# Up stage of a conv FFN: block products for the prompt alone, the sample tokens plainly

## The chip, the cores and the metric

The kernel runs on one core of a Trainium2 chip. The metric is the device time of one execution in microseconds. The kernel before took 1247.82 us (median of three executions, 1247.18 to 1248.13).

## The reference, cut to what matters

One layer of a streaming encoder: a mixer (gated MLP and latent attention), a layer norm, a gated feed-forward part with a causal convolution of width 3, a layer norm. There are 1024 prompt tokens and 8 x 16 = 128 sample tokens, all in float32. The change lies in the product with `w_up`, 1024 rows by 2 x 2816 columns, over all 1152 tokens:

```python
def conv_ffn(x, conv_past, w_up, w_conv, b_conv, w_down):
    up = jnp.einsum('bsd,df->bsf', x, w_up)          # D_MODEL 1024 -> 2 * D_FF = 5632
    padded = jnp.concatenate([conv_past, up], axis=1)
    conv = b_conv
    for k in range(CONV_W):
        conv = conv + w_conv[k] * padded[:, k:k + s_len]
    a, g = jnp.split(conv, 2, axis=-1)
    out = jnp.einsum('bsf,fd->bsd', jax.nn.silu(a) * g, w_down)
```

For the prompt `conv_past` is zero, for the samples it comes as an input. `x` here is the output of the first layer norm.

## The kernel before, in words

**Precision.** Every float32 operand of a large product is split into a high part (rounded by ScalarE, ACT, into the type float32r) and a low part (VectorE, DVE, subtracts: `split`, L59 to L61). A product is then three matmuls: high x high, high x low, low x high.

**Stages.** First the latent attention's projections and the attention (until about 260 us), then the gated MLP (until about 380), then the output projection with the first layer norm (`a4`, L819: nine tiles of 128 tokens, tile 8 holds the samples), then the up stage, then the down stage with the last layer norm.

**From the norm to the up stage.** `a4(t)` leaves the normalised tile t in `yt`; `c4(t)` (L841) transposes it on TensorE (eight transposes, L847) and ACT scales it into `hT` (L855), so that the hidden dimension lies on the partitions. In the loop over t (L940) `c4(t - 1)` stands behind `a4(t)`.

**The up stage.** It goes over 22 strips (L1078). Strip i makes 128 columns of the value half (Ua) and the 128 columns of the gate half that belong to them (Ug): a 2 x 2 block matrix of weights (rows of `w_up` in halves r; Ua or Ug) times a 2 x 2 block matrix of activations (`hblk(q, r, c)`: row half r, token half c of block q). Instead of eight block products it makes seven, in the manner of Strassen and Winograd, from sums and differences of blocks. The products have the numbers 1 to 7. `build_h` (L865) makes the activation operand of a product, once for the whole stage; the ones for 5, 6 and 4 go through one scratch block `Tc`, one after another. `build_w` (L896) makes the weight operand in each strip: a sum or difference on DVE (5, 6, 7, 3), then the split. `product_mm` (L922) runs a product's twelve matmuls: four slices of 128 of the hidden dimension, three matmuls each (L932 to L934). Three PSUM accumulators take the products: X (1, then 6, 7 and 4 on top), Y (2), Z (5, then 3). After each product the state of the accumulator is taken out into U: copied by ACT (1, 5, 6, 4; L1033) or added by DVE (2, 7, 3; L1031).

Before, all 1152 tokens go through the products in two blocks q of 576 tokens, each in two halves of NH = 288 columns: 7 x 2 x 12 matmuls of 288 columns a strip. The samples are the last 128 columns of block 1. The weights' operands have six buffers, so most of a strip's weights are built one strip ahead. In strip 0 the order of products is written out by hand (L1083): four products of block 0, then the two blocks in turn; three products of block 0 (`begun`, L951) are put behind `a4(8)`.

**After a strip.** The convolution of strip i (`conv`, L1035: one pass on ACT, two on DVE, for Ua and Ug), a Silu and the gate product run in pieces between the products of strip i + 1 (`pend`, L1093). The result goes to DRAM (`ad`) and comes back in the down stage. `load_down` (L1063) loads and splits a down operand into the buffers of activation operands that are done with (`ring`), the first four of them during the last strip.

**What sets the order.** The kernel's text gives each engine a stream; a planner with its own idea of durations orders the instructions of each engine, in program order among those it takes for ready, unless `keep_in_program_order` (`pin`) holds them. At run time an engine's queue is in fixed order. A buffer that is taken again waits for its last readers. `raw` tiles of weights have three buffers, U has three, PSUM has eight banks (A 3, B 2, C 1, D 2).

Of the kernel before, what the change touches and what calls it, by code (L numbers as in the profile page):

```python
# [42 lines left out]
def trunk(tc, a, o):  # L43
# [738 lines left out]
    for pl in reversed(g3):  # L782
# [58 lines left out]
    def c4(t):  # L841
        yt = yt_.pop(t)
        for g in range(2):
            tb = bank("B")
            for kk in range(4):
                k = 4 * g + kk
                pe.transpose(tb[:, kk * P:(kk + 1) * P], yt[:, k * P:(k + 1) * P], ident)  # L847
            for kk in range(4):
                k = 4 * g + kk
                lo = t * P  # L850
                while lo < (t + 1) * P:
                    q, at0 = divmod(lo, 2 * NH)
                    n = min((t + 1) * P - lo, 2 * NH - at0)
                    c0 = kk * P + lo - t * P
                    act.activation(hT[q][:, k, at0:at0 + n], tb[:, c0:c0 + n], AF.Identity,  # L855
                                   bias=ln1[:, 1, k:k + 1], scale=ln1[:, 0, k:k + 1])
                    lo += n

    STEPS = (1, 2, 5, 6, 7, 3, 4)
    bops = {}  # L860

    def hblk(q, r, c):
        return hT[q][:, 4 * r:4 * r + 4, c * NH:(c + 1) * NH]

    def build_h(pl, q, s):  # L865
        T = Tc[q]
        if s == 1:
            src = hblk(q, 0, 0)
        elif s == 2:
            src = hblk(q, 1, 0)  # L870
        elif s == 5:
            src = T
            dve.tensor_tensor(T, hblk(q, 0, 1), hblk(q, 0, 0), ALU.subtract)
        elif s == 6:
            src = T
            dve.tensor_tensor(T, hblk(q, 1, 1), T, ALU.subtract)
        elif s == 7:
            src = hblk(q, 0, 1)
            dve.tensor_tensor(src, hblk(q, 1, 1), src, ALU.subtract)
        elif s == 3:  # L880
            src = hblk(q, 1, 1)
        else:
            src = T
            dve.tensor_tensor(T, hblk(q, 1, 0), T, ALU.subtract)
        b = pl.tile([P, 2, 4, NH], F32R, tag=f"b{q}{s}", name=f"b{q}{s}")
        split(b[:, 0], b[:, 1], src)
        bops[q, s] = b
# [8 lines left out]
    def build_w(i, s):  # L896
        A = [[wraw[i][r][:, 512 * c:512 * (c + 1)] for c in range(2)] for r in range(2)]
        if s == 1:
            src = A[0][0]
        elif s == 2:  # L900
            src = A[0][1]
        elif s == 5:
# [19 lines left out]
    def product_mm(i, s, q, hold=lambda x: x):  # L922
        w, h = wops[i, s], bops[q, s]
        key = "Y" if s == 2 else "Z" if s in (5, 3) else "X"
        first = s in (1, 2, 5)
        if first:
            acc[i, q, key] = bank({"X": "A", "Y": "B", "Z": "D"}[key])
        b = acc[i, q, key]
        for k in range(4):
            lh, ll, rh, rl = w[:, 0, k], w[:, 1, k], h[:, 0, k], h[:, 1, k]  # L930
            o_ = b[:, :NH]
            hold(pe.matmul(o_, lh, rh, start=first and k == 0, stop=False, skip_group_check=not first))  # L932
            hold(pe.matmul(o_, lh, rl, start=False, stop=False, skip_group_check=not first))  # L933
            hold(pe.matmul(o_, ll, rh, start=False, stop=k == 3, skip_group_check=not first))  # L934
        return b

    wups = []
    bop0 = None
    begun = {}
    for t in range(TT + 1):  # L940
# [17 lines left out]
        if t == 6:  # L958
# [55 lines left out]
    def out_parts(U, q, c, b):  # L1014
        t0 = (2 * q + c) * NH
        n0 = min(NH, SEQ - t0)
        l = [(U[:, 2 + t0:2 + t0 + n0], b[:, :n0])]
        if n0 < NH:
            l.append((smp_cols(U)[:, :, 2:], b[:, n0:NH].rearrange("p (b s) -> p b s", b=NB)))
        return l  # L1020

    def product(i, s, q):
        b = begun.pop((i, s, q), None)
        if b is None:
            b = product_mm(i, s, q)
# [3 lines left out]
        for dst, src in out_parts(U, q, c, b):  # L1029
            if add:  # L1030
                dve.tensor_tensor(dst, dst, src, ALU.add)  # L1031
            else:
                act.activation(dst, src, AF.Copy)  # L1033
# [27 lines left out]
    ring = [bops[q, s] for s in STEPS for q in range(2)]  # L1061
# [273 lines left out]
```

## Time and profile before

| | us |
|---|---|
| median of three executions | 1247.82 |
| the profiled execution's own time | 1248.44 |
| its span, first to last instruction | 1246.7 |
| TensorE busy | 1227.5 (98%) |
| VectorE busy | 844.6 (68%) |
| ScalarE busy | 533.1 (43%) |
| GpSimd busy | 97.7 (8%) |
| first matmul of the up stage | 469.5 |
| last matmul of the up stage | 972.3 |

The span is 1.7 us shorter than the execution's own time. A matmul's duration in the profile is longer than the distance to the next one, since matmuls overlap in TensorE; a stretch in which TensorE is "busy" all the time may still run faster or slower. In the rows, PE is TensorE, PEld its weight loads, DVE VectorE, ACT ScalarE, POOL GpSimd, SP the engine that issues most DMAs. A group's row has line, engine, operation, output and inputs, shapes and count, then busy time, mean duration in ns, and idle time before it with what ended it.

### The profile page before, as it was taken

To read this page: it belongs to the slowest core of one execution; us is meant where nothing else is said; L and a number is where in the kernel's file an instruction comes from. 1 tells how busy PE (TensorE), PEld (TensorE's weight loads), DVE (VectorE), ACT (ScalarE), POOL (GpSimd) and SP (SyncE) were. 2 spreads that over 40 slices of the span, in tenths; PEclk is the share of its full clock that TensorE was granted. 3 is DMA by queue.
4 is the path that set the end of the run, shared out by engine and by line. 5 is a ranking of instruction groups with operands and counts; after the bars stand their busy time and mean duration, and the time that the engine had idled before them with its cause. 6 is when DMAs were issued, how large, how long until landed. Compare 5 with 4: busy or idle time off the path is not lost.

```text
span 1246.7 us, 19600 instructions
## 1 busy us (share of the span) xinstructions
PE 1227.5 (98%) x7737; PEld 1137.6 (91%) x7737; DVE 844.6 (68%) x1642; ACT 533.1 (43%) x1098; POOL 97.7 (8%) x229
## 2 busy tenths in 40 slices
PE   7999999999999999999999999999999999999997
PEld 7999999889988888999999999999999888888886
DVE  5767888665558568877777677786777794552445
ACT  5335656542134546645445454454545330220332
POOL 0110003200000001111000010000100000000021
PEclk9999999999999999999999999999999999999999
DMA  7201103541043330221222212121233762421012
GB/s 251 83 21 40 33 22 116 165 161 52 1 142 109 134 112 18 104 73 71 90 71 71 74 70 90 63 79 73 71 106 131 291 245 97 145 68 41 12 57 85
DMA packets 35853, 116.47 MB, mean 93 GB/s; under 512 B 5120, under 2 KB 6272, under 8 KB 35760
## 3 DMA queue, kind: packets, MB, share of 16 engines
q1 hardware_dynamic: 30176, 95.19, 22.1%
q0 software_dynamic: 5584, 20.02, 4.3%
q8 instruction: 61, 1.00, 0.3%
q14 instruction: 32, 0.26, 0.1%
HBM read 90.46 MB, written 24.74 MB: 92 GB/s over the span
## 4 chain that ended last, share of the span: by engine, by line
PE 97%; ACT 1%; DVE 1%; DMA 1%; issue 0%; SPq 0%; ACTq 0%; DVEq 0%
PE A L934 8%; PE A L933 7%; PE A L932 7%; PE A L72 7%; PE A L73 7%; PE A L74 7%; PE D L72 7%; PE D L73 7%; PE D L74 7%; PE D L934 4%; PE D L933 4%; PE D L932 4%; PE B L72 2%; PE B L73 2%; PE B L74 2%; PE B L934 2%
## 5 line engine op out<-in xcount | busy, mean ns | idle before, releaser
L932 PE MATMUL A<-b,wu 128*128 128x288 f32 x704 | 207.6, 296 | 0.5 <-DVE U L1031 0.4
L933 PE MATMUL A<-b,wu 128*128 128x288 f32 x704 | 207.9, 296 | 0.0
L934 PE MATMUL A<-b,wu 128*128 128x288 f32 x704 | 206.0, 298 | 0.0
L932 PEld LDWEIGHTS A<-b,wu 128*128 128x128 f32 x704 | 132.4, 188 | 1.0 <-DVE U L1031 0.6
L933 PEld LDWEIGHTS A<-b,wu 128*128 128x128 f32 x704 | 132.8, 189 | 0.0
L934 PEld LDWEIGHTS A<-b,wu 128*128 128x128 f32 x704 | 131.1, 188 | 0.0
L934 PE MATMUL D<-b,wu 128*128 128x288 f32 x352 | 104.8, 298 | 0.0
L932 PE MATMUL D<-b,wu 128*128 128x288 f32 x352 | 104.1, 296 | 0.0
L933 PE MATMUL D<-b,wu 128*128 128x288 f32 x352 | 104.0, 295 | 0.0
L60 ACT ACTIVATE wu<-sc 128x512 fp32r<-128x512 f32 x66 | 41.8, 633 | 138.2 <-PE A L934 105.0
L60 ACT ACTIVATE b<-cbox 128x1024 fp32r<-128x1024 f32 (+1 forms) x40 | 25.6, 676 | 142.7 <-PE B L73 42.2
L61 DVE TENSOR_TENSOR wu<-sc,wu 128x512 fp32r<-128x512 f32 x66 | 46.2, 701 | 46.5 <-ACT wu L60 45.0
L1039 DVE SCALAR_TENSOR_TENSOR cbox<-U,raw,cbox 128x1168 f32<-128x1168 f32 x44 | 63.0, 1431 | 9.4 <-ACT cbox L1038 9.3
L933 PEld LDWEIGHTS D<-b,wu 128*128 128x128 f32 x352 | 66.4, 189 | 0.1
L932 PEld LDWEIGHTS D<-b,wu 128*128 128x128 f32 x352 | 66.1, 188 | 0.3 <-ACT b L60 0.3
L934 PEld LDWEIGHTS D<-b,wu 128*128 128x128 f32 x352 | 66.1, 188 | 0.0
L1040 DVE SCALAR_TENSOR_TENSOR cbox<-U,raw,cbox 128x1168 f32<-128x1168 f32 x44 | 63.0, 1431 | 0.8
L1038 ACT ACTIVATE cbox<-U,raw 128x1168 f32<-128x1168 f32 x44 | 60.0, 1363 | 7.3 <-DVE U L1031 7.1
L60 ACT ACTIVATE wu<-raw 128x512 fp32r<-128x512 f32 x66 | 41.6, 631 | 47.5 <-PE D L934 23.6
L1033 ACT ACTIVATE U<-A 128x288 f32<-128x288 f32 (+2 forms) x154 | 53.0, 368 | 17.5 <-PE A L934 17.5
L61 DVE TENSOR_TENSOR wu<-raw,wu 128x512 fp32r<-128x512 f32 x66 | 45.0, 685 | 14.5 <-ACT wu L60 14.5
L932 PE MATMUL B<-b,wu 128*128 128x288 f32 x176 | 52.1, 296 | 1.7 <-ACT hbox L855 1.7
(449 smaller groups left out, 3419.9 us busy)
## 6 DMA issues: line engine op xcount, KB each, us to landing
raw<-in_w_up SPq DMA_DIRECT2D x44, 512.0 KB, 3.2
ad<-cbox POOLq DMA_DIRECT2D x22, 584.0 KB, 3.1
cbox<-ad SPq DMA_DIRECT2D x22, 584.0 KB, 6.1
raw<-in_w_down SPq DMA_DIRECT2D x22, 512.0 KB, 5.7
xr<-in_xT SPq DMA_DIRECT2D x14, 512.0 KB, 4.1
y<-in_x SPq DMA_DIRECT2D x9, 512.0 KB, 3.6
nd<-y SPq DMA_DIRECT2D x9, 512.0 KB, 2.6
raw<-in_w_uv_in SPq DMA_DIRECT2D x8, 512.0 KB, 4.0
```

The source lines that it names most:

```text
L60: act.activation(hi, src, AF.Copy)
L61: dve.tensor_tensor(lo, src, f(hi), ALU.subtract)
L72: pe.matmul(out, lh, rh, start=first, stop=False)
L73: pe.matmul(out, lh, rl, start=False, stop=False)
L74: pe.matmul(out, ll, rh, start=False, stop=last)
L932: hold(pe.matmul(o_, lh, rh, start=first and k == 0, stop=False, skip_group_check=not first))
L933: hold(pe.matmul(o_, lh, rl, start=False, stop=False, skip_group_check=not first))
L934: hold(pe.matmul(o_, ll, rh, start=False, stop=k == 3, skip_group_check=not first))
L1033: act.activation(dst, src, AF.Copy)
L1038: act.activation(v, U[:, 2:n + 2], AF.Identity, bias=cw[:, fi, 3:4], scale=cw[:, fi, 2:3])
L1039: dve.scalar_tensor_tensor(v, U[:, 1:n + 1], cw[:, fi, 1:2], v, ALU.mult, ALU.add)
L1040: dve.scalar_tensor_tensor(v, U[:, 0:n], cw[:, fi, 0:1], v, ALU.mult, ALU.add)
```

## The change

Only the 1024 prompt tokens go through the seven products, as one block with two halves of NH = 512 columns: 7 x 12 matmuls of 512 columns a strip. The 128 sample tokens are multiplied plainly: the samples' activations are the stationary operand (`hsb`, 2 parts x 8 slices of 128), the moving operand is the weights of one slice for Ua and Ug side by side, 2 x 128 columns; 24 matmuls a strip, in two halves Sa and Sb, into one PSUM bank. Their result has tokens on the partitions, so ACT copies it out, two transposes turn it, and ACT writes it into the sample columns of Ua and Ug.

For that, weights 1 and 2 hold both row halves of Ua and of Ug (`wu1`, `wu2`, one buffer each): product 4 takes its operand from `wu2`. Weights 5, 6, 7 and 3 share a tag with two buffers. One more half-weight is split in each strip. The order of a strip is 1, Sa, 5, 6, 2, 7, Sb, 4, 3 (strip 0: 1, 2, 5, 6, 3, 7, Sa, Sb, 4); weights 6, 2, 7 and 3 of a strip are built within it, 1 and 5 of the next one at its end, and the next strip's raw weights are loaded after product 2. Before the stage, the operands of 1 and 2 are built in the loop over tiles, those of 5, 6, 3 and 7 behind the two begun products 1 and 2, then that of 4 and the samples'. In the down stage the sample columns of the operands are kept in `hsb`, an operand takes one ring buffer of eight instead of two of sixteen, and three of the nine y tiles lie in U's buffers.

The diff, cut to its core:

```diff
-    NH = TT * P // 4
+    NH = SEQ // 2
...
-    hT = [hT0p.tile([P, KD, 2 * NH], F32, tag="hT0", name="hT0"),
-          box[:, :2 * KD * NH].rearrange("p (k i) -> p k i", k=KD)]
-    Tc = [box[:, (2 * KD + 4 * q) * NH:(2 * KD + 4 * q + 4) * NH].rearrange("p (k i) -> p k i", k=4) for q in range(2)]
+    hT = [hT0p.tile([P, KD, NH], F32, tag="hT0", name="hT0"), box[:, :KD * NH].rearrange("p (k i) -> p k i", k=KD)]
+    Tc = box[:, KD * NH:(KD + 4) * NH].rearrange("p (k i) -> p k i", k=4)
+    hsa = box[:, (KD + 4) * NH:].rearrange("p (k i) -> p k i", i=P)
+    hsc = cst.tile([P, 2, P], F32, tag="hs", name="hs")
+    hs32 = [hsa[:, k] for k in range(6)] + [hsc[:, k] for k in range(2)]
...
     def build_w(i, s):
-        if s == 1:
-            src = A[0][0]
-        elif s == 2:
-            src = A[0][1]
-        elif s == 5:
+        if s in (1, 2):
+            w = wup.tile([P, 2, 2, 4, P], F32R, tag=f"wu{s}", name=f"wu{s}")
+            for r in range(2):
+                split(w[:, 0, r], w[:, 1, r], A[r][s - 1].rearrange("p (k i) -> p k i", k=4))
+            wops[i, s] = w
+            return
...
-        w = wups.pop(0) if wups else wup.tile([P, 2, 4, P], F32R, tag="wu", name="wu", bufs=6)
+        w = wup.tile([P, 2, 4, P], F32R, tag="wu", name="wu", bufs=2)
...
         if t == TT:
-            for s in (1, 5, 2):
-                begun[0, s, 0] = product_mm(0, s, 0, tc.keep_in_program_order)
+            for s in (1, 2):
+                begun[0, s] = product_mm(0, s, tc.keep_in_program_order)
+            for pl in reversed(wop):
+                pl.release()
+            bop1 = alloc("bop1")
+            for s in (5, 6, 3, 7):
+                build_h(bop1, s)
         if t > 0:
             c4(t - 1)
...
-            build_h(bop0, 0, 1)
+            build_h(bop0, 1)
             build_w(0, 5)
         if t == 7:
-            build_h(bop0, 0, 2)
-            build_h(bop0, 0, 5)
+            build_h(bop0, 2)
             build_w(0, 6)
-        if t == 8:
-            build_h(bop0, 0, 6)
-            build_w(0, 7)
-            build_w(0, 3)
...
-    for s in (7, 3, 4):
-        build_h(bop1, 0, s)
+    dve.tensor_tensor(Tc, hblk(1, 0), Tc, ALU.subtract)
     hT0p.release()
-    upool = alloc("upool", side="right")
-    for s in (1, 2, 5, 6, 7):
-        build_h(bop1, 1, s)
-    bop2 = alloc("bop2")
-    for s in (3, 4):
-        build_h(bop2, 1, s)
+    upool = alloc("upool")
+    b4 = alloc("b4")
+    hsp = alloc("hsp")
+    build_h(b4, 4)
+    hsb = hsp.tile([P, 2, KD, P], F32R, tag="hsb", name="hsb")
+    split(hsb[:, 0, :6], hsb[:, 1, :6], hsa)
+    split(hsb[:, 0, 6:], hsb[:, 1, 6:], hsc)
...
+    def sample_mm(i, c):
+        if c == 0:
+            acc[i, "S"] = bank("C")
+        o_ = acc[i, "S"][:, :2 * P].rearrange("p (r n) -> p r n", r=2)
+        w = wops[i, 1 + c]
+        for k in range(4):
+            lh, ll, rh, rl = hsb[:, 0, 4 * c + k], hsb[:, 1, 4 * c + k], w[:, 0, :, k], w[:, 1, :, k]
+            pe.matmul(o_, lh, rh, start=c + k == 0, stop=False)
+            pe.matmul(o_, lh, rl, start=False, stop=False)
+            pe.matmul(o_, ll, rh, start=False, stop=c == 1 and k == 3)
+        if c == 1:
+            su = acc[i, "su"] = cst.tile([P, 2 * P], F32, tag="su", name="su")
+            act.activation(su, acc[i, "S"][:, :2 * P], AF.Copy)
+
+    def sample_t(i):
+        su = acc.pop((i, "su"))
+        tb = bank("B")
+        for r in range(2):
+            pe.transpose(tb[:, r * P:(r + 1) * P], su[:, r * P:(r + 1) * P], ident)
+        for r in range(2):
+            act.activation(smp_cols(U_[i][r])[:, :, 2:], tb[:, r * P:(r + 1) * P].rearrange("p (b s) -> p b s", b=NB), AF.Copy)
...
-            order = [(s, q) for s in STEPS for q in range(2)]
+            order = (1, "Sa", 5, 6, 2, 7, "Sb", 4, 3)
...
+            if i == 0:
+                if s == 5:
+                    build_w(0, 3)
+                elif s == 6:
+                    build_w(0, 7)
+            else:
                 if s == 1:
-                    if i:
-                        load_w(i + 1, raw_tile)
-                    build_w(i, 4) if (i, 4) not in wops else None
-                if s != 4:
-                    build_w(i + 1, s)
+                    build_w(i, 6)
+                elif s == "Sa":
+                    build_w(i, 2)
+                elif s == 6:
+                    build_w(i, 7)
+                elif s == 2:
+                    build_w(i, 3)
+                    if not last:
+                        load_w(i + 1, raw_tile)
+            if not last:
+                if s == "Sb":
+                    build_w(i + 1, 1)
+                elif s == 4:
+                    build_w(i + 1, 5)
```

More of the change, by code (lines that the diff above doesn't have):

```diff
@@ L926, in product_mm @@
         if first:
-            acc[i, q, key] = bank({"X": "A", "Y": "B", "Z": "D"}[key])
-        b = acc[i, q, key]
+            acc[i, key] = bank({"X": "A", "Y": "B", "Z": "D"}[key])
+        b = acc[i, key]
         for k in range(4):
             lh, ll, rh, rl = w[:, 0, k], w[:, 1, k], h[:, 0, k], h[:, 1, k]
[L931 to L934, printed above, removed]
-        return b
-    wups = []
-    bop0 = None
+            hold(pe.matmul(b, lh, rh, start=first and k == 0, stop=False, skip_group_check=not first))
+            hold(pe.matmul(b, lh, rl, start=False, stop=False, skip_group_check=not first))
+            hold(pe.matmul(b, ll, rh, start=False, stop=k == 3, skip_group_check=not first))
+        return b
     begun = {}
@@ L1060, in trunk @@
     ops = {}
-    ring = [bops[q, s] for s in STEPS for q in range(2)]
+    ring = [bops[s] for s in (1, 5, 6, 2, 7, 4, 3)]
     def load_down(i):
@@ L1068, in load_down, with rest @@
         hold(sp.dma_start(wr, a["w_down"][i]))
-        ac, wd = (ring[(2 * i + e) % 16].rearrange("p c k i -> p c (k i)") for e in range(2))
-        wd = wd[:, :, :D]
+        r = ring[i % 8].rearrange("p c k i -> p (c k i)")
+        ac, wd = (r[:, e * 2 * SEQ:(e + 1) * 2 * SEQ].rearrange("p (c i) -> p c i", c=2) for e in range(2))
         split(wd[:, 0], wd[:, 1], wr)
-        split(ac[:, 0, :SEQ], ac[:, 1, :SEQ], ra[:, :SEQ])
-        acs = ac[:, :, SEQ:].rearrange("p c (b s) -> p c b s", b=NB)
-        split(acs[:, 0], acs[:, 1], ra[:, SEQ:n].rearrange("p (b s) -> p b s", b=NB)[:, :, 2:])
-        ops[i] = (ac, wd)
+        split(ac[:, 0], ac[:, 1], ra[:, :SEQ])
+        acs = hsb[:, :, i % 8]
+        ops[i] = (ac, acs, wd)
+        def rest():
+            d = acs.rearrange("p c (b s) -> p c b s", b=NB)
+            split(d[:, 0], d[:, 1], ra[:, SEQ:n].rearrange("p (b s) -> p b s", b=NB)[:, :, 2:])
+        if i >= 4:
+            rest()
+        return rest
     pend = []
@@ L1079, in trunk @@
         U_[i] = (new_U(i), new_U(NF + i))
+        last = i + 1 == NF
         if i == 0:
-            q0 = [(s, 0) for s in STEPS]
-            q1 = [(s, 1) for s in STEPS]
-            order = q0[:4] + [x for p in zip(q1, q0[4:]) for x in p] + q1[3:]
             load_w(1, raw_tile)
+            order = (1, 2, 5, 6, 3, 7, "Sa", "Sb", 4)
         else:
-            order = [(s, q) for s in STEPS for q in range(2)]
-        done = {s: 0 for s in STEPS}
-        for s, q in order:
-            if (i, s) not in wops:
-                build_w(i, s)
-            product(i, s, q)
-            done[s] += 1
+            order = (1, "Sa", 5, 6, 2, 7, "Sb", 4, 3)
@@ L1093, in trunk @@
+        late_s = []
+        for s in order:
+            if s == "Sa":
+                sample_mm(i, 0)
+            elif s == "Sb":
+                sample_mm(i, 1)
+            else:
+                product(i, s)
             if pend:
                 pend.pop(0)()
-            if done[s] == 2 and i + 1 < NF:
-                if s == 1:
-                    if i:
-                        load_w(i + 1, raw_tile)
-                    build_w(i, 4) if (i, 4) not in wops else None
-                if s != 4:
-                    build_w(i + 1, s)
@@ L1107, in trunk @@
+            if not last:
[3 more added lines that the diff above has]
+                    build_w(i + 1, 5)
+            elif s in (5, 6, 2, 7):
+                late_s.append(load_down(len(ops)))
+            if s == 4:
+                sample_t(i)
+            if last and s == "Sb":
+                for r in late_s:
+                    r()
+                late_s = []
+        for r in late_s:
+            r()
         while pend:
@@ L1135, in trunk @@
     for t in range(TT):
-        y.append(y2.tile([P, D], F32, tag=f"y{t}", name=f"y{t}") if t < 7 else ctile[t - 4][:, :D])
-    ring += [y2.tile([P, 2, 4, NH], F32R, tag=f"rg{e}", name="rg") for e in range(2)]
+        if t < 4:
+            y.append(y2.tile([P, D], F32, tag=f"y{t}", name=f"y{t}"))
+        elif t < 7:
+            y.append(upool.tile([P, UW], F32, tag="U", name="yU", bufs=3)[:, :D])
+        else:
+            y.append(ctile[t - 4][:, :D])
+    ring.append(y2.tile([P, 2, 4, NH], F32R, tag="rg", name="rg"))
     for t in range(2):
```

101 lines of the change are left out of this document (42 added, 59 removed).

## The prediction

> **What bounds the kernel now.** I read the page's busy line and its chain first, then busy time by stretch, then single instructions in time order.
>
> ```profile
> PE 1227.5 (98%) x7737; PEld 1137.6 (91%) x7737; DVE 844.6 (68%) x1642; ACT 533.1 (43%) x1098; POOL 97.7 (8%) x229
> PE 97%; ACT 1%; DVE 1%; DMA 1%; issue 0%; SPq 0%; ACTq 0%; DVEq 0%
> 468.00:480.00 12.00, 10.33 (x77) 9.89 (x77) 11.31 (x18) 8.74 (x17) 3.99 (x6) 1.00 0.06 22
> 600.00:700.00 100.00, 100.00 (x752) 100.00 (x751) 72.99 (x109) 47.35 (x88) 8.84 (x30) 1.00 0.21 72
> 1030.00:1100.00 70.00, 70.00 (x308) 57.42 (x307) 31.88 (x45) 8.87 (x12) 0.00 (x0) 1.00 0.27 101
> ```
>
> The columns of the last three rows are the stretch, its length, then busy time and count of PE, weight loads, DVE, ACT, POOL, then clock, DMA share and GB/s. TensorE is 97% of the chain that ends last. In the middle of the up stage (600 to 700) it is never free, at a granted clock of 1.00, with DVE at 73% and ACT at 47%. Only where the up stage begins does it stand: 1.67 us between 468 and 480. So two things decide: the time the up stage's matmuls take in sum, and what TensorE waits at the stage's start.
>
> "Busy" counts overlapping durations, so the price of a matmul is the distance between starts. First and last rows of unbroken runs, for 288, 512, 256 columns and the transposes:
>
> ```profile
> 604.97 0.29 PE L932 MATMUL A<-b,wu 128*128 128x288 f32 x1
> 607.10 0.30 PE L933 MATMUL A<-b,wu 128*128 128x288 f32 x1
> ...
> 1099.76 0.39 PE L73 MATMUL A<-b,b 128*128 128x512 f32 x1
> 1103.84 0.39 PE L73 MATMUL C<-b,b 128*128 128x512 f32 x1
> ...
> 314.34 0.28 PE L73 MATMUL D<-xs,wuv 128*128 128x256 f32 x1
> 317.92 0.29 PE L73 MATMUL D<-xs,wuv 128*128 128x256 f32 x1
> ...
> 479.43 1.03 PE L847 MATMUL B<-ident,y 128*128 128x128 f32 x8
> 480.22 0.38 PE L934 MATMUL A<-b,wu 128*128 128x288 f32 x1
> 480.44 0.30 PE L932 MATMUL D<-b,wu 128*128 128x288 f32 x1
> ```
>
> 16 steps of 288 columns take 2.13 us, 133.1 ns each; 18 of 512 take 4.08, 226.7 ns; 30 of 256 take 3.58, 119.3 ns. A line through these is 0.416 ns a column plus 13 ns a matmul. Eight transposes and one 288-column matmul take 1.01 us (479.43 to 480.44): 0.11 us a transpose.
>
> **The change, part 1: the matmuls.** The stage has 22 strips. Before, each has 7 products x 2 blocks x 12 matmuls of 288 columns.
>
> ```profile
> L932 PE MATMUL A<-b,wu 128*128 128x288 f32 x704 | 207.6, 296 | 0.5 <-DVE U L1031 0.4
> L932 PE MATMUL D<-b,wu 128*128 128x288 f32 x352 | 104.1, 296 | 0.0
> L932 PE MATMUL B<-b,wu 128*128 128x288 f32 x176 | 52.1, 296 | 1.7 <-ACT hbox L855 1.7
> ```
>
> Three such lines of code make 3 x (704 + 352 + 176) = 3696; at 133.1 ns, 491.9 us. After: 22 x 7 x 12 = 1848 of 512 columns, 418.9 us; 22 x 24 = 528 of 256 columns for the sample tokens, 63.0 us; 44 transposes, 4.8 us. Sum 486.7 us, a gain of 5.2 us. The columns in fact rise (1,064,448 to 1,081,344, +7.0 us at 0.416); it is 1320 matmuls fewer at 13 ns (-17.2) that pay for them and for the transposes.
>
> [...]
>
> Two prices are not shown. The sample's moving operand is two runs of 128 columns with a gap between them: 119.3 ns if the gap is free, and if it costs a second start, 2 x (0.416 x 128 + 13) = 132.6, 7.0 us more in all. I take 119.3, since the instruction is one. And 512 columns do not run at 226.7 everywhere:
>
> ```profile
> 308.66 0.40 PE L72 MATMUL A<-wuv,xs 128*128 128x512 f32 x1
> 313.99 0.40 PE L74 MATMUL A<-wuv,xs 128*128 128x512 f32 x1
> ```
>
> 23 steps take 5.33 us, 231.7 ns. At that pace the prompt's products would cost 9.2 us more. The up stage's 288-column steps fit the line of the faster run, so I take 226.7.
>
> **Part 2: the start of the stage.** Here the change costs. Before, block 0 (tokens 0 to 575) has operands ready early and feeds TensorE while block 1 is prepared. After, only products 1 and 2 (tokens 0 to 511) can be prepared early; 5, 6, 3 and 7 need tokens 512 to 1023, product 4 follows 6 through the shared Tc.
>
> ```profile
> 461.30:468.20 6.90, 0.00 (x0) 1.00 0.19 76
> 468.26 0.69 DVE L834 SCALAR_TENSOR_TENSOR y<-y,A 128x512 f32<-128x512 f32 x1 [7.04 <-PE A L74]
> 468.75 1.03 PE L847 MATMUL B<-ident,y 128*128 128x128 f32 x8
> 469.54 0.38 PE L932 MATMUL A<-b,wu 128*128 128x288 f32 x1
> 473.24 2.88 ACT L855 ACTIVATE hbox<-B,ln 128x128 f32<-128x128 f32 x8
> 474.78 0.40 PE L932 MATMUL B<-b,wu 128*128 128x288 f32 x1 [1.67 <-ACT hbox L855]
> 481.60 1.36 DVE L873 TENSOR_TENSOR hbox<-hbox 128x1152 f32<-128x1152 f32 x1 [1.78 <-ACT hbox L855]
> 486.84 0.40 PE A L932
> L61 DVE TENSOR_TENSOR b<-raw,b 128x1024 fp32r<-128x1024 f32 x20 | 24.4, 1221 | 2.5 <-ACT b L60 2.5
> L61 DVE TENSOR_TENSOR wu<-raw,wu 128x512 fp32r<-128x512 f32 x66 | 45.0, 685 | 14.5 <-ACT wu L60 14.5
> L60 ACT ACTIVATE b<-raw 128x1024 fp32r<-128x1024 f32 x20 | 21.1, 1056 | 4.8 <-DMA raw<-in_w_down 4.8
> L60 ACT ACTIVATE wu<-raw 128x512 fp32r<-128x512 f32 x66 | 41.6, 631 | 47.5 <-PE D L934 23.6
> ```
>
> DVE goes from 685 ns at 512 columns to 1221 at 1024, so an operand of 2048 takes about 1.22 + 1.07 = 2.3 us; ACT from 631 to 1056, so 1.9. (My estimates; before, the same work came in pieces of 1152 at 1.35.) The transposes of tile 7 stand at 468.75, ACT needs 0.36 a piece (2.88 for 8): its first four pieces end near 470.8, all at 472.2. DVE meanwhile does the last tile's layer norm up to about 471.4. Then, taking what is ready in program order:
>
> - DVE: difference for 5 to 473.7, rest of the norm to 474.8, low part of 3 to 477.1, of 5 to 479.4 (ACT's high parts came at 474.1 and 476.0), difference for 6 to 481.7, for 7 to 484.0, low of 6 to 486.3, of 7 to 488.6, difference for 4 to 490.9, product 2's add and the low parts of weights 3 and 7 (0.7 each) to 493.0, low of 4 to 495.3, the sample's split to 496.7.
> - TensorE: products 1 and 2 from 469.5 to 474.9 (12 x 0.2267 = 2.72 each), the last tile's transposes (0.9), product 5 from 479.5, 6 from 486.4, 3 from 492.4 (its weights share a buffer with 5's, so they are split after 5 has run), 7 to 497.8, the samples (24 x 0.1193 = 2.9) to 500.7, 4 and the strip's two transposes to 503.6.
>
> That is 34.1 us for 23.0 us of work: 11.1 us of waiting, where before 1.67 (474.78) and a few tenths more (the chain's gap ahead of 486.84), 2.0 in all, were lost. Cost: 9.1 us. Strip 1 cannot fill the hole: its weights 1 and 2 have one buffer each, held until the samples and product 4 of strip 0 have read them. Bounds: if every small DVE piece falls best, DVE's nine operand passes (20.7), norm rest and two weight splits (2.5) end at 494.6 and, with the sample's split (1.4) and product 4, the strip at 498.9: waiting 6.4. If the weights of 3 and 7 are split only after all operands, product 3 starts near 497.5 and the strip ends near 508: waiting 15.
>
> **Part 3: within a strip.** DVE splits one more half-weight (0.69) and makes 3 adds of 512 instead of 8 over 288 columns:
>
> ```profile
> L1031 DVE TENSOR_TENSOR U<-U,B 128x288 f32<-128x288 f32 x44 | 19.6, 446 | 0.0
> L1156 DVE TENSOR_TENSOR y<-y,B 128x512 f32<-128x512 f32 x13 | 8.9, 686 | 18.6 <-PE B L74 18.6
> L1038 ACT ACTIVATE cbox<-U,raw 128x1168 f32<-128x1168 f32 x44 | 60.0, 1363 | 7.3 <-DVE U L1031 7.1
> L1039 DVE SCALAR_TENSOR_TENSOR cbox<-U,raw,cbox 128x1168 f32<-128x1168 f32 x44 | 63.0, 1431 | 9.4 <-ACT cbox L1038 9.3
> raw<-in_w_up SPq DMA_DIRECT2D x44, 512.0 KB, 3.2
> ```
>
> About 3.0 us of adds (446 ns, a little less for the parted pieces) become 2.1; DVE stays near 16 us of a 22.1 us strip. It is hidden by the matmuls as now. Waits that are new: weights 1 and 2 in one buffer, the others in two. Weights 6 of a strip may be written when product 3 of the last one ends, and are wanted 2.72 + 1.43 + 2.72 = 6.9 us later; the split takes 1.3 and a queue place. The next strip's second raw half lands 3.2 us after weights 3 and 7 let go of it, some 13 of 22 us into the strip. The convolution of Ua now starts after product 3, the strip's last, and takes 1.4 + 2 x 1.4 us; the next strip's Ug has that buffer and is first written by 5's eviction, 6.9 us in, while product 3, which needs that eviction done, comes 19 us in. Behind an ACT or DVE instruction that waits stand the evictions, and TensorE after them. I take 0, at most 0.2 us a strip (4 us): half of one split's slip beyond the slack. In the last strip DVE splits weights 6, 2, 7 and 3 beside the first four down operands, 5.5 us more (4 x 1.38); TensorE has eight PSUM banks of partial sums to go on with. I take 0, at most 3.
>
> **Sum.** The profiled execution took 1248.44 (span 1246.7 and 1.7 around it). -5.2 + 9.1 = +3.9: 1252.3. The median shown is 0.6 lower than that execution, so 1251.7.
>
> **The rivals.**
>
> (a) The start is covered after all: faster. Tile 7 is normalised by 461.3, and DVE then stands for 6.9 us (the first row of part 2's fence). If its transposes go in ahead of tile 8's last matmuls, two differences (4.6 us) move into that hole, product 5 starts near 474, and waiting falls by 5.7 to between 0.7 and 5.4, say 3: -5.2 + 1 = -4.2, 1243.6. Against it: before, those transposes came only behind tile 8's matmuls. It decides from waiting under 4.7 us on.
>
> (b) Gain and loss meet: best fall of DVE's pieces, waiting 6.4 to 8: -0.8 to +0.8, 1247.5. For it: the planner does mix small pieces in now.
>
> (c) The small buffers bite in every strip: +4 us over my sum, and a start as in the forecast: 1255.7, with the start's upper bound 1259.6.
>
> (d) The matmuls do not get cheaper: the pace of 231.7 or a second start inside the sample's operand, +7.0 to +9.2: 1259.8 in the middle. Against it, the line through three sizes. [...]
>
> **How the numbers follow.** Forecast 0.42, (a) 0.14, (b) 0.22, (c) 0.13, (d) 0.09. About 0.2% (2.5 us) is what a measurement tells from no change: faster is (a), 0.14; same is (b), 0.22; slower the rest, 0.64. The range takes in (b), most of (c) and the upper bound of the start, and the upper half of (a): 1244 to 1259. The forecast's own range is 1250 to 1255.
>
> **What would show it.** Steps of 512-column matmuls near 227 ns and sample steps near 119 in mid-stage; the distance from the first matmul of strip 1 to the first of strip 21 about 20 x 22.1 us. At the stage's start, gaps of TensorE released by DVE's or ACT's write of a b tile, ahead of products 5, 6, 3, and a first strip of about 34 us. I am wrong if those gaps sum to under 5 us, if mid-stage strips take 22.4 us or more, or if TensorE waits for a wu tile in strip after strip.

## The result and the profile after

The changed kernel takes 1260.3 us (median of 4 runs, 1260.20 to 1260.41) against 1247.5 for the kernel before in the same session: a ratio of 1.010, 95% interval 1.0085 to 1.012. It is slower, as forecast, but by three times the forecast amount (1251.7), and outside the range. Two executions of the kernels that are tried below took far longer than all others (5913.7 us with a pad of 992 bytes, 2058.0 us with both pads and the transposes moved) and are left out of their medians.

The page of the changed kernel, its busy line and its chain of waits; then busy time by stretch, with the columns of the prediction (stretch, length, busy time and count of PE, weight loads, DVE, ACT, POOL, then clock, DMA share, GB/s):

```profile
PE 1234.4 (98%) x6461; PEld 1057.5 (84%) x6461; DVE 843.0 (67%) x1545; ACT 537.2 (43%) x1041; POOL 130.5 (10%) x229
PE 93%; DVE 4%; DMA 1%; ACT 1%; issue 1%; SPq 0%; DVEq 0%; ACTq 0%
470.00:480.00 10.00, 4.78 (x19) 3.38 (x18) 9.96 (x9) 6.78 (x7) 0.00 (x0) 0.83 0.00 0
476.60:483.40 6.80, 3.90 (x9) 3.13 (x10) 6.80 (x6) 0.21 (x2) 0.00 (x0) 0.50 0.00 0
600.00:700.00 100.00, 100.00 (x489) 83.06 (x488) 74.27 (x90) 48.33 (x80) 15.16 (x31) 1.00 0.23 82
```

1276 instructions of TensorE are gone, and its share of the chain falls from 97 to 93%, with DVE at 4. At the stage's start (470 to 480) TensorE works 4.78 us of 10 while DVE never stands; and there is a thing that the prediction didn't have, a granted clock of 0.50 for 6.8 us. In the middle of the stage (600 to 700) TensorE is as full as before, at a clock of 1.00. So what is lost there is not waiting but the length of a step.

Single instructions in time order, first the start of the stage, then one whole product in mid-stage (first rows of two neighbouring products, 12 steps apart), then matmuls one strip period apart, 17 strips between the two, in the kernel before and in the changed one, and last a wait in the down stage:

```profile
467.93 0.48 PE L930 MATMUL A<-b,wu 128*128 128x512 f32 x1
474.98 0.50 PE L930 MATMUL D<-b,wu 128*128 128x512 f32 x1 [1.20 <-ACT b L60]
479.50 0.79 PE L931 MATMUL D<-b,wu 128*128 128x512 f32 x1 [4.03 <-DVE b L61]
488.30 0.50 PE L931 MATMUL A<-b,wu 128*128 128x512 f32 x1 [0.59 <-DVE b L61]
497.35 0.39 PE L1029 MATMUL C<-wu,hsb 128*128 128x256 f32 x1 [0.38 <-DVE hsb L61]
...
712.83 0.39 PE L930 MATMUL A<-b,wu 128*128 128x512 f32 x1
715.63 0.39 PE L930 MATMUL B<-b,wu 128*128 128x512 f32 x1
...
570.32 0.28 PE L1027 MATMUL C<-wu,hsb 128*128 128x256 f32 x1
953.82 0.28 PE L1027 MATMUL C<-wu,hsb 128*128 128x256 f32 x1
...
1019.66 0.39 PE L74 MATMUL A<-b 128*128 128x512 f32 x1
1021.52 0.47 PE L72 MATMUL A<-b 128*128 128x512 f32 x1 [1.47 <-DVE yU L1192]
```

```profile
563.34 0.30 PE L933 MATMUL A<-b,wu 128*128 128x288 f32 x1
944.37 0.30 PE L933 MATMUL A<-b,wu 128*128 128x288 f32 x1
```

- The waits at the start are those that were foreseen: for ACT's and DVE's writes of the b tiles ahead of products 5 and 6, and for the sample's operand. Over the whole start the distances between TensorE's starts hold 11.4 us more than the work at full pace; by the same count it was 3.4 before. 1.6 of the 11.4 is the lowered clock: eight steps between 480 and 483.4 are 0.43 us apart instead of 0.23.
- 12 steps from 712.83 to 715.63 take 2.80 us, 233.3 ns each, not 226.7.
- 17 strips take 383.50 us, 22.56 each; before they took 381.03, 22.41 each. The strips were to become 0.24 us shorter and became 0.15 longer.
- In the down stage a step of 0.23 us takes 1.86 (1019.66 to 1021.52): DVE is late with a sum.

The 11.9 us between the spans (1258.6 and 1246.7) thus lie: the stage begins 1.6 us earlier (467.93 against 469.54); from there to the marker of strip 4 +8.6; the 17 strips +2.5; from the marker of the last strip to the end +2.4, of which about 1.1 is that wait (it loses 1.6 us, and the kernel before loses 0.5 at 1021.10). The other 1.3 us were not traced.

### The profile page after: what moved, and what is told of

Read it like the earlier page. It is cut to its first block, busy times and chain, and to the rows that moved or that the text cites. A ratio compares the mean times of both kernels' runs of the same rounds, so it can differ in the third digit from the quotient of the medians.

```text
span 1258.6 us, 16935 instructions
## 1 busy us (share of the span) xinstructions
PE 1234.4 (98%) x6461; PEld 1057.5 (84%) x6461; DVE 843.0 (67%) x1545; ACT 537.2 (43%) x1041; POOL 130.5 (10%) x229
## 4 chain that ended last, share of the span: by engine, by line
PE 93%; DVE 4%; DMA 1%; ACT 1%; issue 1%; SPq 0%; DVEq 0%; ACTq 0%
PE A L72 7%; PE A L73 6%; PE A L74 6%; PE A L931 6%; PE A L932 6%; PE A L930 6%; PE D L72 6%; PE D L73 6%; PE D L74 6%; PE D L932 3%; PE D L930 3%; PE D L931 3%; PE B L74 2%; PE B L72 2%; PE B L73 2%; PE C L74 2%
## 5 line engine op out<-in xcount | busy, mean ns | idle before, releaser
L931 PE MATMUL A<-b,wu 128*128 128x512 f32 x352 | 138.6, 394 | 0.6 <-DVE b L61 0.6
L930 PE MATMUL A<-b,wu 128*128 128x512 f32 x352 | 138.8, 395 | 0.0
L932 PE MATMUL A<-b,wu 128*128 128x512 f32 x352 | 136.3, 395 | 0.0
L932 PEld LDWEIGHTS A<-b,wu 128*128 128x128 f32 x352 | 66.0, 188 | 15.6
L931 PEld LDWEIGHTS A<-b,wu 128*128 128x128 f32 x352 | 66.1, 188 | 15.1 <-DVE b L61 1.0
L930 PEld LDWEIGHTS A<-b,wu 128*128 128x128 f32 x352 | 65.9, 188 | 14.5 <-ACT b L60 0.2
L60 ACT ACTIVATE b<-cbox 128x1024 fp32r<-128x1024 f32 x20 | 20.6, 1055 | 125.9 <-PE B L73 36.7
L931 PE MATMUL D<-b,wu 128*128 128x512 f32 x176 | 70.3, 400 | 4.0 <-DVE b L61 4.0
L930 PE MATMUL D<-b,wu 128*128 128x512 f32 x176 | 70.6, 401 | 1.7 <-ACT b L60 1.2
L932 PE MATMUL D<-b,wu 128*128 128x512 f32 x176 | 71.5, 406 | 0.0
L61 DVE TENSOR_TENSOR wu<-raw,wu 128x512 fp32r<-128x512 f32 x88 | 58.0, 683 | 9.0 <-ACT wu L60 8.7
L1016 DVE TENSOR_TENSOR U<-U,A 128x512 f32<-128x512 f32 x22 | 15.1, 689 | 67.7 <-PE A L932 67.7
L60 ACT ACTIVATE wu<-raw 128x512 fp32r<-128x512 f32 x88 | 52.3, 624 | 15.2 <-DMA raw<-in_w_up 11.5
L1018 ACT ACTIVATE U<-A 128x512 f32<-128x512 f32 x66 | 39.4, 598 | 37.6 <-PE A L932 36.7
L1004 POOL COPY U<-raw 128x16 f32<-128x16 f32 x44 | 50.4, 1146 | 0.0
L1029 PE MATMUL C<-wu,hsb 128*128 128x256 f32 x176 | 49.3, 280 | 0.4 <-DVE hsb L61 0.4
L1027 PE MATMUL C<-wu,hsb 128*128 128x256 f32 x176 | 49.3, 280 | 0.0
L1028 PE MATMUL C<-wu,hsb 128*128 128x256 f32 x176 | 49.2, 280 | 0.0
```

The lines of the kernel that those rows point to most:

```text
L60: act.activation(hi, src, AF.Copy)
L61: dve.tensor_tensor(lo, src, f(hi), ALU.subtract)
L930: hold(pe.matmul(b, lh, rh, start=first and k == 0, stop=False, skip_group_check=not first))
L931: hold(pe.matmul(b, lh, rl, start=False, stop=False, skip_group_check=not first))
L932: hold(pe.matmul(b, ll, rh, start=False, stop=k == 3, skip_group_check=not first))
L1004: pool.tensor_copy(smp_cols(U)[:, :, 0:2], stt[:, fi])
```

## The experiments

### What a step of 512 columns costs

The changed kernel's other stages run 512 columns at 226.7 ns and at 231 to 233. In the up stage's trace the slow pace did not go with what the other engines did: the mean is 232.6 ns over the steps in which DVE and ACT both worked and 233.3 where neither did. What was left was where the two operands lie in SBUF, so blocks of bare matmuls were put in front of the kernel, each group of 60 on a line of its own (the code in short):

```
+    X = xb.tile([P, 55288], F32R)        # at_byte(b, n): n columns of X from byte b of the partition
+    for (lh, ll, rh, rl) of UP(moving byte, stationary byte, columns, ...), 5 times 12:
+        pe.matmul(pb, lh, rh); pe.matmul(pb, lh, rl); pe.matmul(pb, ll, rh)
```

> The kernel after, with a block put in front of it: 34 groups of 60 matmuls on one big tile, each group with its own line, all other engines idle, the same pattern of 12 (4 x hi*hi, hi*lo, lo*hi) as a product. The groups differ in the byte address of the moving operand (that of b1, 52224, and of b4, 164640) and of the stationary one (that of wu, wu1, wu2, or 84992 plus 0, 32, 64, 128, 256, 480, 512, 992, 1024), in the layout (up stage, down stage, one address only) and in the columns (512, 384, 288, 256). Theory A, the pace depends on how the two addresses stand to one another: the group with b1 and wu takes 233 ns a matmul as in the up stage of after, the group at plus 0 takes 226.7, and the series of offsets shows the modulus. Rival B, the slow pace comes from what else runs in the up stage: every group of 512 columns takes 226.7. Rival C, it comes from the layout of the stationary operand (pieces of 512 bytes side by side): all groups in the up layout take 233, only the down layout 226.7. At 288 columns the up stage before took 133.1: by A and C I expect that group to show no difference, since that stage had the same wu addresses.

Its timeline, one row a group; the distance from one row's start to the next, divided by 60, is the pace. Lines 157 to 159 are the stationary addresses 84992 plus 480, 512 and 992 with the moving operand at b1's place; 163 is b1 with wu1's place, 164 is b4's place with wu's; 176 to 179 are 288 and 256 columns, at plus 0 and at wu's place in turn, and 180 and 181 likewise 384 columns. Two operands are said to agree when their byte addresses leave the same remainder modulo 256:

```profile
156.47 14.15 PE L157 MATMUL A<-X 128*128 128x512 f32 x60
170.46 13.77 PE L158 MATMUL A<-X 128*128 128x512 f32 x60
184.07 14.15 PE L159 MATMUL A<-X 128*128 128x512 f32 x60
198.06 13.76 PE L160 MATMUL A<-X 128*128 128x512 f32 x60
...
239.27 14.16 PE L163 MATMUL A<-X 128*128 128x512 f32 x60
253.27 13.89 PE L164 MATMUL A<-X 128*128 128x512 f32 x60
267.00 13.89 PE L165 MATMUL A<-X 128*128 128x512 f32 x60
...
418.52 8.15 PE L176 MATMUL A<-X 128*128 128x288 f32 x60
426.51 8.20 PE L177 MATMUL A<-X 128*128 128x288 f32 x60
434.55 7.35 PE L178 MATMUL A<-X 128*128 128x256 f32 x60
441.74 7.17 PE L179 MATMUL A<-X 128*128 128x256 f32 x60
448.75 10.57 PE L180 MATMUL A<-X 128*128 128x384 f32 x60
```

The group at plus 512 takes 13.61 us (226.8 ns a step), those at plus 480 and 992 take 13.99 (233.2); b1 with wu1 14.00 (233.3), b4 with wu 13.73 (228.8). DVE and GpSimd stand, and the layout is the same throughout, so rivals B and C fall: it is the addresses. The groups in the down stage's layout show the same two paces (lines 172 and 173: 13.63 us agreeing, 13.99 not). Plus 0, 256, 512 and 1024 end at 226.7, plus 32, 64 and 128 take 232.6 to 233.3, so the modulus is 256. b1 and its like begin at 0 modulo 256, b4 and hsb at 32, all wu tiles at 224.

The other sizes say more. With agreeing operands 256, 384 and 512 columns take 119.8, 173.5 (448.75 to 459.16) and 226.7 ns: close to the prediction's line, 0.418 a column plus 13 a matmul. With b1 and wu they take 116.8, 176.5 (459.16 to 469.75) and 233.3: by the two ends 0.455 a column and next to nothing a matmul, though 384 lies 1.5 ns above that line. So between 256 and 384 columns the order of the two is reversed. The two groups of 288 columns, 133.2 and 134.0, are no such pair. A slice of 288 columns is 1152 bytes, 4.5 times 256, so the slices of the moving operand begin at 0 and 128 in turn, and the group at plus 0 agrees in half of its steps only; the group at wu's place agrees in none. My expectation of no difference at 288 was nearly right (0.8 ns), but 288 columns that agree throughout were not run, and a tile of such slices as the kernel before has cannot agree throughout.

Whose address must agree was tried in a second block, with moving and stationary offsets that alternate, and a finer row of offsets.

```
+    AL(moving offsets, stationary offsets): matmul i takes m[i % len(m)] and s[i % len(s)]
+    AL([0, 32], [0, 32])    AL([0, 32], [32, 0])    AL([0], [4]) ... AL([0], [32] * 12 + [0] * 48)
```

> A second block of groups of 60 matmuls of 512 columns in front of the kernel after, all other engines idle; the moving operands begin at 52224 plus a multiple of 4096 plus m, the stationary ones at 84992 plus a multiple of 512 plus s (both 0 modulo 256 where m and s are 0). Whose address is it that must agree with the moving operand's: its own stationary operand's, or that of the next matmul, which is loaded meanwhile? Groups with m and s going 0, 32, 0, 32 together (own agree, next not) and crosswise (own not, next agree). Theory A (the load that runs beside the stream): crosswise takes 226.7 ns, together 233. Rival B (a matmul and its own operand): the other way round. Then s - m from 4 to 256 bytes: by the groups so far 256 takes 226.7, 32, 64 and 128 take 232.5 to 233.4 and 192 (64 short of 256) 228.8; I expect values between for the rest and no other fast one. Last, 12 matmuls that disagree ahead of 48 that agree, and 1 ahead of 59: from the strips with pads I expect some 8 matmuls until 226.7 is regained.

Its rows: all agree (149), own agree and next not (150), own not and next agree (151), none agree (152), then s - m = 252 and 256 (170, 171), each with the row that follows:

```profile
42.59 13.76 PE L149 MATMUL A<-X 128*128 128x512 f32 x60
56.19 14.08 PE L150 MATMUL A<-X 128*128 128x512 f32 x60
70.11 13.96 PE L151 MATMUL A<-X 128*128 128x512 f32 x60
83.91 14.15 PE L152 MATMUL A<-X 128*128 128x512 f32 x60
97.89 13.79 PE L153 MATMUL A<-X 128*128 128x512 f32 x60
...
334.36 13.77 PE L170 MATMUL A<-X 128*128 128x512 f32 x60
347.96 13.79 PE L171 MATMUL A<-X 128*128 128x512 f32 x60
361.59 13.85 PE L172 MATMUL A<-X 128*128 128x512 f32 x60
```

The step takes 226.7 ns when all agree; 232.0 when only a matmul and its own operand do, 230.0 when only the next one's does, 233.0 for none. Both theories of whose address counts fall: a mixture of two residues is slow either way. Of 17 offsets under 256 only 252 is as fast as 256; 192 takes 229.0, the others 228 to 234. Behind a disagreeing group the slow pace lasted some steps: 153 shows 227.3 over its 60 and 256 shows 227.2, by my estimate the surplus of four to six slow steps. The group with 12 disagreeing steps ahead took 13.69 us (361.59 to 375.28), by the same count two steps more than its 12, not the eight I expected. Why the pace goes by the two addresses stays open.

Does it hold in the kernel? Unused tiles shift the operands.

```
     hsc = cst.tile([P, 2, P], F32, tag="hs", name="hs")
+    cst.tile([P, 248], F32, tag="pad", name="pad")       # 992 bytes; 8 columns for 32 bytes
```

> One unused tile of 992 bytes a partition ahead of the operands, so that b1, b2, b5, b6, b3 and b7 begin at 2016 modulo 2048 as the wu tiles do; nothing else changes. Theory A (addresses): the up stage's matmuls of 512 columns go from 233 to about 227 ns, mid-stage strips from 22.43 to about 22.0 us, and the time falls by about 10 us, to 1250. Rival B (the stage) or C (the layout): 233 ns stay and the time is 1260 within 2 us.

> The same with 32 bytes: the b tiles then agree with the wu tiles modulo 64 but not modulo 512. Theory A with a small modulus (64): 227 ns and 1250 us, as with 992 bytes. Theory A with a larger one: something between, as product 4 of after (b4 and wu2 agree modulo 64, 229.8 ns), so 229 to 230 ns and about 1254 us. Rival B or C: 233 ns and 1260 us.

992 bytes: 1255.7 us, ratio to before 1.0067 (1.005 to 1.0084). 32 bytes: 1258.8, 1.009 (1.0075 to 1.0105). A gain, but less than half of what was expected of the first. Its rows, product 4 (first) and products 5 and 6, with the row that follows each:

```profile
704.65 0.39 PE L931 MATMUL A<-b,wu 128*128 128x512 f32 x1
707.45 0.28 PE L1029 MATMUL C<-wu,hsb 128*128 128x256 f32 x1
708.75 0.40 PE L931 MATMUL D<-b,wu 128*128 128x512 f32 x1
711.53 0.39 PE L931 MATMUL A<-b,wu 128*128 128x512 f32 x1
714.25 0.39 PE L931 MATMUL B<-b,wu 128*128 128x512 f32 x1
```

Product 6 is fast (2.72 us for 12 steps), product 4 slow (2.80: b4 now begins at 0, its weights at 224), and product 5, which follows samples at a disagreeing hsb, takes 2.78, though its own operands agree: the steps behind a disagreeing group are slow too. With 32 bytes the b tiles and wu agree modulo 64 and differ by 192 modulo 256; a modulus of 64 is excluded. A difference of 192 takes 229 ns in the block, by which I expected about 1254 us. The 17 strips shortened by 0.09 us each, to 22.47, where 229 ns in six of the seven products would by my estimate give some 0.25; why they did not is open. The next trial makes all operands agree:

```
             bop0 = alloc("bop0")
+            bop0.tile([P, 248], F32, tag="pad", name="pad")
     upool = alloc("upool")
+    upool.tile([P, 56], F32, tag="pad", name="pad4")
```

> Two unused tiles, 992 bytes in front of b1 and 224 bytes in front of b4, so that all seven b tiles and hsb begin at 224 modulo 256 as all wu tiles do; earlier stages keep their addresses. Theory (the pace goes by the two addresses modulo 256, and after an interruption at other addresses some eight matmuls pass before it is regained): all 84 matmuls of 512 columns in a mid-stage strip run at 226.7 ns and none of them slowly, the 24 of the samples at 119.8 instead of 117; 84 x 0.2267 + 24 x 0.1198 + 0.2 for the transposes = 22.1 us a strip instead of 22.5; the time falls by 7 to 9 us, to about 1252. Rival: the mixing of products and samples costs the slow pace whatever the addresses (with 992 bytes alone, where b4 and hsb did not agree, products 5, 1 and 3 kept 229 to 231 ns): 22.35 us a strip and 1256 as there.

1253.0 us, ratio 1.0039 (1.0025 to 1.0053): 7.3 us under the changed kernel, with 1.2 KB of SBUF a partition and no instruction. Rows: product 6, and the two strip markers as above:

```profile
709.47 0.39 PE L930 MATMUL A<-b,wu 128*128 128x512 f32 x1
712.19 0.39 PE L930 MATMUL B<-b,wu 128*128 128x512 f32 x1
...
569.11 0.28 PE L1029 MATMUL C<-wu,hsb 128*128 128x256 f32 x1
947.35 0.28 PE L1029 MATMUL C<-wu,hsb 128*128 128x256 f32 x1
```

2.72 us for 12 steps, 226.7 ns; 17 strips in 378.24 us, 22.25 each, 0.31 less than after and 0.16 less than before. The strips are still 0.1 us over the expected 22.1. The first five steps of 512 columns behind a group of samples take 228 to 236 ns here too, so a change between products and samples costs something even where all agree.

### What the start of the stage costs

First DVE's share: four of its nine operand passes left out.

```
-            dve.tensor_tensor(Tc, hblk(0, 1), hblk(0, 0), ALU.subtract)      # and likewise for 6, 7 and 4
+            src = hblk(0, 1)
```

> Leaves out the four differences of DVE over 2048 columns at the stage's start (products 5, 6, 7 and 4 read plain blocks of the tokens, so their operands are wrong); copies and low parts stay. Theory: the first strip waits for DVE's chain of nine operand passes, four of them gone (9.2 us): TensorE's gaps there fall from 8.9 us to 3 or less, the clock is not lowered, strip 0 takes 25 to 27 us instead of 34.5, and the time falls by 7 to 10 us, to 1250 to 1253. Rival: the transposes of the last tile, ACT's passes or the two buffers of the weights hold it: less than 4 us of gain.

1254.8 us, 5.5 under the changed kernel; ratio 1.0057 (1.004 to 1.0073). One stretch of the same start:

```profile
470.00:480.00 10.00, 7.94 (x32) 5.59 (x31) 7.57 (x6) 9.37 (x10) 0.00 (x0) 1.00 0.00 0
```

TensorE's loss at the start falls from 11.4 us to 5.3 and the clock stays at 1.00, so most of what TensorE waits for there is DVE's chain. The gain is between theory and rival: with DVE relieved, ACT is the full engine (9.37 of 10 us).

Is the lowered clock a cost of its own? Idle matmuls keep TensorE at work in the hole.

```
+            fill = bank("C")
+            for _ in range(18):
+                tc.keep_in_program_order(pe.matmul(fill, wops[0, 1][:, 0, 0, 0], bops[1][:, 0, 0], start=True, stop=True))
```

> After, with 18 idle matmuls of 512 columns (b1 and wu1 into a free bank, never read) pinned between product 2 and product 5, where TensorE stands for 1.2 and 4.0 us. Theory: the standing is what lowers the granted clock, so the clock stays at 1.00 and product 5's matmuls take 233 ns instead of 427; but the end of strip 0 is set by DVE's chain and not by TensorE, so the time stays within 1 us of 1260.3. Rival: the 1.6 us of slow matmuls are paid for in full, and the time falls by 1.5 to 2 us.

1262.0 us, ratio 1.0119 (1.0105 to 1.0132). The interval overlaps that of the changed kernel (1.0102, 1.0085 to 1.012), but the median is 1.7 us higher where at most 1 was expected. Its stretches at the hole and later, and the longest of the waits that follow:

```profile
475.00:480.00 5.00, 3.71 (x17) 2.68 (x15) 5.00 (x4) 2.20 (x3) 0.00 (x0) 1.00 0.00 0
490.00:500.00 10.00, 7.74 (x31) 5.88 (x30) 8.11 (x10) 5.64 (x10) 0.00 (x0) 0.83 0.14 53
...
493.74 0.52 PE L1030 MATMUL C<-wu,hsb 128*128 128x256 f32 x1 [2.20 <-ACT hsb L60]
```

The clock is not lowered at the hole any more (1.00), and no time is won. Product 6's second step comes 20.4 us after the stage's first matmul in both kernels (488.71 after 468.33 here, 488.30 after 467.93 in the changed kernel), so what product 5 saves is waited away ahead of it: the 1.6 us lie under the chain of passes. The clock is lowered later instead (0.83 over 490 to 500), behind the wait of 2.20 us for the sample's operand, so a start without any lowered clock was not seen in this run.

Can the chain be shortened without changing the result? Three ways were tried. One gives two differences to GpSimd and lets 6 go to a block that is dead.

```
+            T6 = hblk(0, 0)
+            dve.tensor_tensor(T6, hblk(1, 1), Tc, ALU.subtract)
+            pool.tensor_tensor(hblk(0, 1), hblk(1, 1), hblk(0, 1), ALU.subtract)     # 7
+            pool.tensor_tensor(Tc, hblk(1, 0), T6, ALU.subtract)                     # 4
```

> The chain at the stage's start is parted: the difference for 6 goes to the dead block of tokens 0 to 511 instead of over the difference for 5, the differences for 7 and 4 go to GpSimd; the result is computed as before, and no pad is in. Theory (strip 0 waits for DVE's chain of operand passes): two of nine passes (4.6 us) leave DVE, 6 no longer waits for 5's split; product 6 starts near 481.5 instead of 486, strip 0 ends 5 to 7 us earlier and the time is about 1254. The clock is lowered as in after, if about 4 us of standing is what lowers it. Rival: GpSimd's passes of 2048 columns (about 4.6 us each, by the 2.3 us for 1024 in the last stage) are late for 7 and 4 or slow DVE down while they run: a gain of under 3 us.

> The pads of the one and the parted chain of the other together. If the pace in the strips and the waiting at the start are two separate terms, the gains add: 1260.3 - 8 - 6 = about 1246, the same as or a little faster than before. If a faster TensorE only waits longer for DVE at the start, the gain of the pads is about 0.4 us smaller there, not more.

1265.2 us (1.0139, 1.0125 to 1.0153) and with the pads 1257.9 (1.008, 1.0066 to 1.0094): worse by 4.9 in both. The rows of GpSimd, then of DVE and TensorE, without the pads:

```profile
472.29 6.55 POOL L959 TENSOR_TENSOR hbox<-hbox 128x2048 f32<-128x2048 f32 x1 [4.37 <-DVE rv L85]
...
472.17 2.29 DVE L957 TENSOR_TENSOR hT<-hbox 128x2048 f32<-128x2048 f32 x1
474.50 6.48 DVE L61 TENSOR_TENSOR b<-hbox,b 128x2048 fp32r<-128x2048 f32 x1
483.84 0.79 PE L931 MATMUL D<-b,wu 128*128 128x512 f32 x1 [6.29 <-DVE b L61]
```

GpSimd's pass, issued while DVE's of 2.29 us runs to 474.46, ends at 478.84; DVE's next, of the same size, is issued at 474.50 and ends at 480.98, 2.14 us after GpSimd's. So DVE's pass took 6.48 us beside GpSimd's where the one before it took 2.29, and TensorE waits 6.29 us for DVE's next pass behind it. Why the one slows the other these rows don't show. The pads still give 7.3 us here: pace and start are separate terms.

The next puts the transposes of tile 7 between the halves of tile 8's matmuls, which is rival (a) by hand.

```
         elif t == NP:
+            a4(t, tc.keep_in_program_order, lambda: c4(NP - 1, tc.keep_in_program_order))
```

> The transposes of tile 7 are put, by a fixed order, between the two halves of tile 8's matmuls (tile 7 is normalised some 6 us before those end), and the difference for 6 goes to the dead block of tokens 0 to 511; no pad, GpSimd is not used; the result is computed as before. This is rival (a) of the prediction done by hand. Theory (DVE's chain sets the end of strip 0): the three differences for 5, 6 and 7 (6.9 us) fall into the 6.9 us in which DVE stood, so the chain ends 5 to 6 us earlier; strip 0 ends near 497 instead of 502.4, product 5 doesn't wait, and the time is 1260.3 - 5.5 = about 1255. Rival: the eight transposes in the middle hold up tile 8 and product 1 by as much, and the waits move to products 3 and 4: a gain of under 2 us.

> The same with the two pads. If pace and start are separate terms: 1253.0 - 5.5 = 1247.5, level with before; over 1250 if the rival of the run without pads holds.

1262.5 us (1.0123, 1.0105 to 1.0141), with the pads 1253.1 (1.0049, 1.0035 to 1.0063): no gain over 1260.3 and 1253.0. Product 5's long wait is gone, but ACT and TensorE now show, without the pads:

```profile
495.71 1.94 ACT L60 ACTIVATE b<-hbox 128x2048 fp32r<-128x2048 f32 x1
497.70 0.50 PE L932 MATMUL A<-b,wu 128*128 128x512 f32 x1 [1.68 <-ACT b L60]
```

Tile 8's norm fell behind the operand passes, so its transposes came after product 7, and ACT's pass for product 4, whose operand DVE had ready at 484.2, stands in its queue behind them until 495.71. The wait moved to the end of strip 0. So, last, a written order for that too:

```
+            bsplit(5, Tc); y_rest(); bsplit(6, hblk(0, 0)); bsplit(3, hblk(1, 1))
+            c4(NP, kp, kp)
+            kp(dve.tensor_tensor(hblk(0, 1), hblk(1, 1), hblk(0, 1), ALU.subtract)); bsplit(7, hblk(0, 1))
```

> The pads, the transposes of tile 7 in the middle of tile 8's matmuls as before this, and now a fixed order on DVE and ACT for the rest of the chain, so that tile 8's norm and its transposes come right after product 5 and nothing stands in ACT's queue before them: difference 5, 6, tile 8's norm, low parts of 5, 6, 3, difference 7, low part of 7, difference 4, the sample's split, low part of 4. Computed as before. Theory (the runs before only moved the wait to tile 8's transposes, behind which ACT's passes for 4 and the sample stood): DVE's chain now ends near 493 and strip 0 near 496.5 against 503 in after; time 1253.0 - 6 = about 1247, level with the kernel before, and the clock stays at 1.00. Rival: another queue place (weights of 3 and 7, evictions) takes the wait over once more: 1250 or more.

1250.6 us (11 executions, 1246.6 to 1255.5), ratio 1.0025 (1.0014 to 1.0037): 2.4 us under the pads alone where 6 were expected, and still a little slower than before. In its trace TensorE's loss at the start is 8.8 us, about 3.2 of it at a lowered clock that the theory had excluded:

```profile
490.70 0.50 PE L945 MATMUL A<-b,wu 128*128 128x512 f32 x1 [1.08 <-DVE b L973]
...
477.70:481.10 3.40, 3.40 (x9) 2.63 (x9) 3.40 (x3) 0.28 (x1) 0.00 (x0) 0.51 0.39 151
491.40:494.80 3.40, 3.40 (x10) 2.66 (x9) 2.65 (x3) 1.86 (x3) 0.00 (x0) 0.51 0.00 0
```

No version that was tried beats the kernel before. Other addresses in the kernel before were not tried.

## Why the prediction was wrong

- **Part 1, the price of 512 columns: the step that failed.** It took 226.7 ns and named 231.7 as the other bound; the stage runs at 233.3 (products with a b tile at 0) and 229 to 230 (product 4). Seen from the block of groups, the line was fitted through points of different kinds: 512 columns from the down stage, whose operands agree modulo 256, 288 from the up stage before, whose operands don't. "The up stage's 288-column steps fit the line" was the argument for 226.7, and it could not decide: by the prediction's own prices a line through 119.3, 133.1 and 231.7 (0.440 a column plus 6.3) misses none of the three by more than 0.3 ns. Over 17 strips this turned a gain of 4.0 us into a loss of 2.5, some 6.5 of the 8.0 us by which the sum was short (11.9 us between the spans, 3.9 forecast); the pads give 7.3 us back.
- **Part 1, the rest.** The sample's parted operand costs no second start: its steps took 116 to 118 ns. Fewer and wider matmuls saved nothing at these addresses: the 17 strips took 2.5 us more.
- **Part 2, the start: right.** Forecast waiting 11.1 us, measured 11.4; cost over before 9.1 forecast, 8.0 measured, since the start before lost 3.4 us by this count and not the 2.0 that the prediction had read. Product 5 was to run from 479.5 and did (479.50), product 6 from 486.4, and ran from 488.30; the estimated passes of 2.3 us on DVE and 1.9 on ACT measured 2.29 and 1.9. The forecast did not have the lowered clock; its 1.6 us are in the 11.4 and lie under DVE's chain, so that the two sums are so near is in part luck.
- **Part 3: right within a strip, wrong behind it.** TensorE waits for no wu tile in mid-stage. The last strip and the down stage lost 2.4 us where 0 was taken and 3 was the bound; the cause of about half of that stays open.
- **The rivals.** (a) needs more than transposes moved: done by hand it moved the wait. (b) and (c) did not happen. (d) did, in its first half: its 231.7 comes near the 233.3 that was measured; I gave it 0.09 on a line through three sizes. The middle of its +7.0 to +9.2 gave 1259.8; measured 1260.3. That it is so near is in part luck, since the second start in the sample's operand did not happen and 2.4 us came from behind the stage.

Of what the prediction said would make it wrong, one came true: mid-stage strips of 22.4 us or more (22.56).

## What to carry to other kernels

Here the price of a matmul went by its size and by a pair of addresses (226.7 or 233.3 ns at 512 columns, 119.8 or 116.8 at 256): take it from a step with the operands that the changed step will have, or print where the tiles lie and compare them modulo 256, slice by slice. If steps of one shape show two paces in one trace, find the cause before choosing one; here the slower was in the prediction as a bound, and the price was worth most of the error. Where the last input of a stage feeds a chain of passes on one engine, work out the chain's length: with four of DVE's nine passes left out TensorE's loss at the start fell from 11.4 to 5.3 us. A stall removed at one place can come up at the next one in some engine's queue: with tile 7's transposes moved ahead, ACT's pass for product 4 stood until 495.71 and the time was 1262.5 us against 1260.3.

## What the runs showed of the hardware

- **TensorE and addresses.** In the blocks a stream of 512 columns of fp32r took 226.7 ns a step when moving and stationary operands agreed modulo 256 bytes and mostly 228 to 234 when they didn't (at 252 bytes 226.7); at 256 columns the order was the reverse, 119.8 and 116.8. So in these runs the place of the weights shows in the pace.
- **The clock.** It stood at 0.50 for 6.8 us in the changed kernel, from within the wait of 4.03 us on, and at 0.51 for 3.4 us at a time in the last version above. There it fell at 491.4 though the longest wait named in the ten microseconds before was 1.08 us; with the four differences left out, where the longest named wait was 0.86 us, it stayed at 1.00. Which waits, or what sum of them, lower it, these runs don't show.
- **GpSimd beside DVE.** Beside a pass of GpSimd over 2048 columns a pass of DVE that used nothing of it took 6.48 us, where the same pass in the changed kernel took 2.28; with two of nine passes moved to GpSimd the kernel became 4.9 us slower.
